# A two-layer encoder on one core: hi-weight products first, wide weight tiles, one kind of buffer, and an earlier gate convolution

## The chip, the cores and the metric

The kernel runs on one core of one Trainium2 chip. The metric is the device time of one execution in microseconds, the median of three runs. PE is the matrix engine (its weight loads are shown as PEld), ACT the scalar engine, DVE the vector engine, POOL the general one, and SP the queue that issues most transfers.

## The reference

Two layers on 256 tokens of width 2048, all in float32:

```
h = rms_norm(x, norm1_g[l])
q, k, v, gu, gv = jnp.split(h @ w_in[l], splits, axis=-1)
attn = banded_window_attention(q, k, v, sink[l])
sgu = chunked_spatial_gating(gelu(gu), gelu(gv), ...)
mixed = concatenate([rms_norm(attn, ...), rms_norm(sgu, ...)])
x = x + mixed @ w_o[l]
a = depthwise_conv_centred(rms_norm(x, norm2_g[l]) @ w_up[l], conv_w[l], conv_b[l])
g, u = jnp.split(a, 2, axis=-1)
x = x + (silu(g) * u) @ w_down[l]
```

The inner width of the last part is 5632, 44 tiles of 128 channels.

## The kernel before, in words

**Products in three parts.** PE multiplies in a fast 32-bit format that rounds its inputs. So each weight tile and each activation is split into a rounded part, hi, and the rest, lo, and a product is made of three: activation hi by weight hi, activation lo by weight hi, activation hi by weight lo. A block is four row tiles (KB = 4) of 512 weight columns: one transfer of 1 MB to `raw`, then `split_weights` has ACT round it to `hi` (L127) and DVE subtract it to `lo` (L111), each in two tiles of 1024 columns. `rows_by_cols` then issues 24 matmuls (L170), 128x512 each: for each of the four row tiles the four hi products (two halves of the tokens, two activation parts), then the two low ones.

**gu, the one projection made the other way.** `unit` takes the weights as the stationary operand and 256 channels a call: 32 hi products of 512 columns (L211), then 32 low ones of 256 (L216). `joined` then adds the two halves of its PSUM tile: ACT copies one (L227), DVE adds (L229). That frees the PSUM tile; there are three such tiles, `mm`.

**Stages of a layer.** Keys and queries, the second query group, gv in two chunks, gu in four units, with the steps of attention and of the spatial gating let in between; then w_o in two halves of four output columns; then up and down. In the last part the 44 tiles are worked off in two halves, 24 and 20. In each, `gate_and_up` makes for every four tiles a gate and an up product (L170 again); `leave` scales the result (L799), lays its 16-bit words apart (L801) and has the DMA queue transpose them; some blocks later `up_in` joins the words (L381), convolves gate and up (`convolved`, L781 to L785), multiplies and splits the result (`split_plain`, L242 and L243) into the list `ys`. Then four output columns of the down-projection run over `ys`, four tiles a block.

**What sets the order.** A scheduler orders the instructions of each engine when the program is made; each engine then works them off in that order and waits by semaphores. Weight splitting, joins and the like are `urgent`: first among what is ready. A tile of a pool can be taken only when an older tile of the pool has been released by its last reader; the scheduler places an instruction with that in view. Pools before: 58 general buffers `slots` of 2 KB a partition, 4 of the same size for evacuated results (`evp`), 4 for scratch (`scr`), 3 `raw` of 8 KB, 4 `hi` and 4 `lo` of 4 KB. `let_in` and `take` put waiting steps behind a given matmul.

## Time and profile before

| | us |
|---|---|
| median of three runs | 1971.58 |
| lowest, highest | 1971.37, 1972.12 |
| the profiled execution: its own time | 1971.57 |
| its span, first to last instruction | 1969.8 |
| PE busy | 1963.6 |
| ACT, DVE busy | 1316.6, 1256.4 |

The page is read as follows: a group of instructions has its line, engine, operation, output and inputs, shape and count, then its busy time and the mean of one in ns, then the engine's idle time just before them and what ended it. A timeline row has start, duration, engine, line, operation and count; times are us from the span's start. A waits row has the engine that waited, what for, the us in total, how often, and the longest.

### The profile page before, as it was taken

The page shows a single profiled execution, that of the slowest core. Times are in us where ns is not written, and L with a number is a line of the kernel's source. Part 1 is how long each engine was busy: PE and PEld are TensorE (multiplying, and loading weights), DVE is VectorE, ACT ScalarE, POOL GpSimd, SP SyncE. Part 2 cuts the span into 40 slices and gives each one's busy share as a digit, 9 for nine tenths or more (in the row PEclk, how much of TensorE's full clock was granted, in tenths as well). Part 3 has the DMA queues.
Part 4 walks back from the last instruction along what each step waited for, and adds up shares of the span by engine and source line. Part 5 has one row for each costly group of instructions (what it writes and reads, how often), then busy time and mean ns, then how long its engine had stood idle before and what let it go on. Part 6 is the DMA issues. An engine that isn't in the chain of part 4 may idle for free.

```text
span 1969.8 us, 23916 instructions
## 1 busy us (share of the span) xinstructions
PE 1963.6 (100%) x8880; PEld 1630.6 (83%) x8880; DVE 1256.4 (64%) x1754; ACT 1316.6 (67%) x1685; POOL 22.6 (1%) x25
## 2 busy tenths in 40 slices
PE   9999999999999999999999999999999999999999
PEld 8888888888888888888888888888888888888887
DVE  6779776666664456666567796666666544666664
ACT  6687487877753477777666864787777435777742
POOL 0100000000000000000000000000000000000000
PEclk9999999999999999999999999999999999999999
DMA  9764687777755677776667456867776556678763
GB/s 342 205 204 150 205 239 202 222 219 228 216 198 192 199 215 204 229 221 205 215 204 248 141 178 203 235 206 218 232 218 219 193 192 203 213 216 217 220 216 126
DMA packets 190741, 414.09 MB, mean 210 GB/s; under 512 B 139424, under 2 KB 140704, under 8 KB 145568
## 3 DMA queue, kind: packets, MB, share of 16 engines
q1 hardware_dynamic: 189904, 411.83, 67.2%
q8 instruction: 69, 1.13, 0.2%
q10 hardware_dynamic: 720, 0.73, 0.1%
q14 instruction: 48, 0.39, 0.1%
HBM read 378.43 MB, written 2.10 MB: 193 GB/s over the span
## 4 chain that ended last, share of the span: by engine, by line
PE 97%; DVE 2%; issue 0%; DMA 0%; SPq 0%; POOL 0%; ACT 0%; DVEq 0%
PE mm L170 91%; PE mm L211 2%; PE tp L170 1%; PE mm L216 1%; DVE lo L111 1%; PE tp L254 0%; PE tp L256 0%; PE tp L255 0%; PE tp L697 0%; PE tp L482 0%; DMA raw<-in_w_in 0%; DVE sl L235 0%; DVE xr L562 0%; SPq L87 0%; DVE sl L265 0%
## 5 line engine op out<-in xcount | busy, mean ns | idle before, releaser
L170 PE MATMUL mm<-hi,sl 128*128 128x512 f32 x5296 | 1418.4, 389 | 0.8 <-DVE sl L243 0.6
L111 DVE TENSOR_TENSOR lo<-raw,hi 128x1024 fp32r<-128x1024 f32 (+1 forms) x708 | 856.5, 1217 | 627.6 <-ACT hi L127 616.7
L170 PEld LDWEIGHTS mm<-hi,sl 128*128 128x128 f32 x5296 | 992.7, 188 | 208.2 <-DVE sl L243 1.5
L127 ACT ACTIVATE hi<-raw 128x1024 fp32r<-128x1024 f32 (+1 forms) x708 | 739.9, 1051 | 461.5 <-PE mm L170 426.0
L170 PE MATMUL mm<-lo,sl 128*128 128x512 f32 x2648 | 816.1, 389 | 0.0
L170 PEld LDWEIGHTS mm<-lo,sl 128*128 128x128 f32 x2648 | 496.9, 188 | 103.1
L381 ACT COPY sl<-sl 128x1024 uint16<-128x1024 uint16 x98 | 132.1, 1351 | 119.3 <-DMA sl<-sl 119.2
L781 ACT ACTIVATE sc<-sl,pc 128x256 f32<-128x256 f32 x176 | 97.0, 588 | 0.0
L801 ACT COPY sl<-ev 128x1024 uint16<-128x1024 uint16 x88 | 89.5, 1037 | 0.0
L782 DVE SCALAR_TENSOR_TENSOR sc<-sl,pc,sc 128x255 f32<-128x255 f32 x176 | 79.1, 479 | 2.6 <-ACT sc L781 2.6
L785 DVE SCALAR_TENSOR_TENSOR sc<-sl,pc,sc 128x255 f32<-128x255 f32 x176 | 79.1, 480 | 1.6
L211 PE MATMUL mm<-sl,hi 128*128 128x512 f32 x256 | 62.0, 391 | 0.0
L211 PEld LDWEIGHTS mm<-sl,hi 128*128 128x128 f32 x256 | 47.3, 188 | 9.3
L799 ACT ACTIVATE ev<-mm,yr 128x512 f32<-128x512 f32 x88 | 54.8, 672 | 0.0
L235 DVE SCALAR_TENSOR_TENSOR sl<-sl,pc 128x256 fp32r<-128x256 f32 x96 | 42.5, 479 | 16.9 <-ACT sl L234 16.9
L242 ACT ACTIVATE sl<-sl 128x256 fp32r<-128x256 f32 x88 | 32.1, 410 | 27.9 <-DVE sl L827 27.4
L234 ACT ACTIVATE sl<-sl,pc 128x256 fp32r<-128x256 f32 x96 | 43.0, 496 | 1.2 <-DMA pc<-in_pcol 0.6
L535 ACT COPY sl<-sl 128x1024 uint16<-128x1024 uint16 x24 | 32.4, 1349 | 6.8 <-DMA sl<-sl 6.8
L216 PE MATMUL mm<-sl,lo 128*128 128x256 f32 x256 | 34.2, 285 | 0.0
L243 DVE TENSOR_TENSOR sl<-sl 128x256 fp32r<-128x256 f32 x88 | 33.3, 419 | 0.0
L216 PEld LDWEIGHTS mm<-sl,lo 128*128 128x128 f32 x256 | 32.4, 191 | 0.6
L827 DVE TENSOR_TENSOR sl<-sl,sc 128x512 f32<-128x512 f32 x44 | 30.2, 686 | 0.2
(112 smaller groups left out, 582.7 us busy)
## 6 DMA issues: line engine op xcount, KB each, us to landing
raw<-in_w_up SPq DMA_DIRECT2D x176, 1024.0 KB, 5.0
raw<-in_w_down SPq DMA_DIRECT2D x88, 1024.0 KB, 4.9
raw<-in_w_in SPq DMA_DIRECT2D x38, 1024.0 KB, 5.3
raw<-in_w_o SPq DMA_DIRECT2D x32, 1024.0 KB, 5.0
raw<-in_w_gu SPq DMA_DIRECT2D x16, 1024.0 KB, 5.1
sl<-sl SPq DMA_TRANSPOSE x244, 3.6
sl<-in_prow SPq DMA_DIRECT2D x12, 256.0 KB, 7.0
raw<-in_w_in SPq DMA_DIRECT2D x8, 256.0 KB, 4.9
```

Source lines behind the costliest of these rows:

```text
L111: nc.vector.tensor_tensor(out=lo, in0=part, in1=hi.bitcast(F32), op=ALU.subtract)
L127: nc.scalar.activation(hi[:, cs], part, AF.Copy)
L170: nc.tensor.matmul(ps[m], acts[kk][:, part % 2, m * P : (m + 1) * P], w, start=first and kk == 0 and part == 0, stop=last and kk == KB - 1 ...
L211: nc.tensor.matmul(ps[:, i, :], tile_of(his, k, i), x1, start=k == 0, stop=False)
L216: nc.tensor.matmul(ps[:, i, :SEQ], tile_of(los, k, i), acts[k][:, 0, :], start=False, stop=k == NK - 1)
L234: nc.scalar.activation(t[:, 0, :], src, AF.Copy, scale=g)
L381: nc.scalar.copy(words, tall.rearrange("p (b a) n -> p b (a n)", b=2))
L781: nc.scalar.activation(t[:, i, :], s[:, i, :], AF.Identity, bias=col(3), scale=col(1))
L782: nc.vector.scalar_tensor_tensor(out=t[:, i, 1:], in0=s[:, i, : SEQ - 1], scalar=col(0), in1=t[:, i, 1:], op0=ALU.mult, op1=ALU.add)
L785: nc.vector.scalar_tensor_tensor(out=t[:, i, : SEQ - 1], in0=s[:, i, 1:], scalar=col(2), in1=t[:, i, : SEQ - 1], op0=ALU.mult, op1=ALU.add)
L799: nc.scalar.activation(rows, ps[:, m, :], AF.Copy, scale=r2[:, m : m + 1])
L801: nc.scalar.copy(h, rows.bitcast(U16).rearrange("p (j n b) -> p j b n", j=2, b=2))
```

## The change

The diff has five live parts.

1. **Order of the products.** In `rows_by_cols`, and in a new function `direct` for the down-projection, a block issues its 16 hi products first and its 8 low ones last. In `unit` the low products go row tile by row tile, the two channel halves in turn.
2. **Wide tiles.** `hi` and `lo` are one tile of 2048 columns a block, three `hi` and two `lo`; one rounding and one subtraction of 2048 columns take the place of two of 1024 (narrower for the first blocks of layer 0, by `step`).
3. **One kind of general buffer.** `evp` and `scr` are gone; what they held is taken from `slots`, now 62.
4. **Gate's convolution.** `gate_in` joins gate's words, convolves them and applies silu at once; `up_in` does the same for up alone.
5. **The halves and w_down.** The halves are 20 and 24 tiles. w_down lies in the order of its use, one long row a partition; the transfers keep their size.

New functions for a way of multiplying 2x2 blocks with seven products (`seven`, `seven_out`, `mixed`) come with it, but the table that would call for them, `FAST`, is empty, so none of it is issued.

```diff
+HALVES = ((0, 20), (20, NF))
+FAST = ((), ())
...
-    slots = pool("slots", 58)
-    evp = pool("evp", 4)
+    slots = pool("slots", 62)
     rawp = pool("rawp", 3)
-    hip = pool("hip", 4)
-    lop = pool("lop", 4)
-    scr = pool("scr", 4)
+    hip = pool("hip", 3)
+    lop = pool("lop", 2)
...
     def ev():
-        return evp.tile([P, 2, SEQ], F32, tag="ev", name="ev")
+        return sl([P, 2, SEQ])
 
     def sc(shape):
-        return scr.tile(shape, F32, tag="sc", name="sc")
+        return sl(shape)
...
+            hi, lo = hi_tile(), lo_tile()
+            for a in range(0, n, step):
+                cs = slice(a, min(a + step, n))
+                nc.scalar.activation(hi[:, cs], raw[:, cs], AF.Copy)
+                lo_part(lo[:, cs], raw[:, cs], hi[:, cs])
+        return hi, lo
...
                 product(m, kk, 0)
                 product(m, kk, 1)
-            for m in range(2):
-                product(m, kk, 2)
             if kk == 1:
                 let_in()
+        for kk in range(KB):
+            for m in range(2):
+                product(m, kk, 2)
...
-        for i in range(2):
-            for k in range(NK):
+        for k in range(NK):
+            for i in range(2):
                 nc.tensor.matmul(
                     ps[:, i, :SEQ], tile_of(los, k, i), acts[k][:, 0, :], start=False, stop=k == NK - 1
                 )
-                if i == 0 and k == 1:
-                    take(steps)
+            if k == 0:
+                take(steps)
...
+            step = 4 * W if l or b > 1 else W if raw is not None else 2 * W
+            rows_by_cols(ps, acts[b * KB : b * KB + KB], src, b == 0, b == NB - 1, raw, step=step)
...
             def gate_in(tall):
-                g.extend(together(t) for t in tall)
+                for i in range(2):
+                    g = together(tall[i])
+                    y = sl([P, 2, SEQ])
+                    nc.scalar.activation(y, convolved(g, 4 * j + 2 * i), AF.Silu)
+                    gs.append(y)
...
-                    y = sl([P, 2, SEQ])
-                    nc.scalar.activation(y, convolved(g[i], f), AF.Silu)
-                    t = convolved(u, NF + f)
+                    y = gs[i]
+                    t = convolved(u, NF + 4 * j + 2 * i)
...
-        for f0, f1 in ((0, 24), (24, NF)):
-            ys = []
+        w_at = 0
+        for half, (f0, f1) in enumerate(HALVES):
+            ys, plain = [], {}
...
-                    src = w_down[l, c, :, k * W : (k + KB) * W]
-                    rows_by_cols(ps, ys[k - f0 : k - f0 + KB], src, k == f0, k + KB == f1, None, end and k + KB == f1)
...
+                    src = w_down[l, :, w_at : w_at + len(cs) * len(ks) * W]
+                    w_at += len(cs) * len(ks) * W
+                    acts = [ys[k - f0] for k in ks]
...
+                    direct(sums[c], acts, src, fresh[c], finished, end and finished)
```

Lines move with the change: L170 is now L185 (L213 in `direct`), L127 is L158, L111 is L146, L211 and L216 are L329 and L334, L227 and L229 are L345 and L347, L242 and L243 are L360 and L361, L249 is L367, L482 is L600.

**PE, the first two blocks of the program** (`mm` is the PSUM tile, `sl` the activations). Before:

```order
L170 MATMUL mm<-hi,sl 128x512 x4
L170 MATMUL mm<-lo,sl 128x512 x2
L170 MATMUL mm<-hi,sl 128x512 x4
L170 MATMUL mm<-lo,sl 128x512 x2
L170 MATMUL mm<-hi,sl 128x512 x4
```

Now:

```order
L124 MATMUL tp<-ones 128x128 x10
L185 MATMUL mm<-hi,sl 128x512 x16
L185 MATMUL mm<-lo,sl 128x512 x8
L185 MATMUL mm<-hi,sl 128x512 x16
L185 MATMUL mm<-lo,sl 128x512 x8
```

The low products of all four row tiles have moved behind the last hi one.

**DVE, layer 0, where gu ends and w_o begins** (`lo_...` are low weights, those of 1024 or 2048 columns; `ev_1662<-mm_1549`, `sl_1456<-mm_1321` are joins of gu units). Before, at the end of the third unit, `mm_1549`:

```order
L714 TENSOR_SCALAR sl_1235<-sl_1235,mv_1239,lnr_1244 128x512
L111 TENSOR_TENSOR lo_1695<-raw_1692,hi_1694 128x1024
L111 TENSOR_TENSOR lo_1699<-raw_1692,hi_1698 128x1024
L229 TENSOR_TENSOR ev_1662<-mm_1549,ev_1660 128x512
L111 TENSOR_TENSOR lo_1705<-raw_1702,hi_1704 128x1024
L687 TENSOR_TENSOR ev_1662<-ev_1662,rb_750 128x512
L111 TENSOR_TENSOR lo_1709<-raw_1702,hi_1708 128x1024
```

Now, at the end of the fourth unit, `mm_1601`; `mm_1321` is the second one:

```order
L146 TENSOR_TENSOR lo_1744<-raw_1741,hi_1743 128x2048
L586 TENSOR_TENSOR rs_1393<-rs_1393,es_1391 128x4
L383 TENSOR_TENSOR sl_489<-sl_489,sl_1415 128x512
L146 TENSOR_TENSOR lo_1790<-raw_1787,hi_1789 128x2048
L347 TENSOR_TENSOR sl_1456<-mm_1321,sl_1454 128x512
L588 RECIPROCAL rec_1400<-rs_1393 128x4
L353 SCALAR_TENSOR_TENSOR sl_1418<-sl_1413,pc_83,sl_1418 128x256
L806 TENSOR_TENSOR sl_1456<-sl_1456,rb_708 128x512
L592 TENSOR_SCALAR sl_1370<-sl_1370,rec_1400 128x256 x2
L592 TENSOR_SCALAR sl_1380<-sl_1380,rec_1400 128x256 x2
L353 SCALAR_TENSOR_TENSOR sl_1421<-sl_1413,pc_83,sl_1421 128x256
L367 TENSOR_TENSOR sl_1520<-tp_1514,sl_1519 128x512
```

The join of the second unit has moved from the second unit's end to the fourth's, behind two low tiles. `lo_1744` and `lo_1790` take over the buffers of `lo_1605` and `lo_1611`, so they wait for PE's last product on these. On PE the same place reads now (`[waits ...]` names the engine whose semaphore the row waits for):

```order
L334 MATMUL mm_1601<-sl_225,lo_1605 128x256 x2
L334 MATMUL mm_1601<-sl_299,lo_1611 128x256 x2
L334 MATMUL mm_1601<-sl_302,lo_1611 128x256 x2
L334 MATMUL mm_1601<-sl_307,lo_1611 128x256 x2
L334 MATMUL mm_1601<-sl_310,lo_1611 128x256 x2
L334 MATMUL mm_1601<-sl_375,lo_1611 128x256 x2
L334 MATMUL mm_1601<-sl_378,lo_1611 128x256 x2
L334 MATMUL mm_1601<-sl_383,lo_1611 128x256
L600 MATMUL tp_1523<-ident_116,sl_1230 128x128 [waits Activation_49]
L600 MATMUL tp_1523<-ident_116,sl_1230 128x128
L600 MATMUL tp_1523<-ident_116,sl_1240 128x128 x2
L334 MATMUL mm_1601<-sl_383,lo_1611 128x256
```

Behind these rows stand the last two low products on `lo_1611` and then the first of w_o, `mm_1740<-hi_1743,sl_1159`, which waits for the join of `mm_1321`.

**PE, layer 0, the end of the first up-projection** (`mm_4023` and `mm_4212` are the first two output columns of the down-projection, `sl_4142` is the first of the last four `y`, `hi_4182` its weights). Now:

```order
L213 MATMUL mm_4212<-hi_4215,sl_2846 128x512 [waits Activation_49]
L213 MATMUL mm_4212<-hi_4215,sl_2846 128x512 x2
L213 MATMUL mm_4023<-hi_4182,sl_4142 128x512 [waits Activation_49]
L213 MATMUL mm_4212<-hi_4215,sl_2846 128x512
L213 MATMUL mm_4212<-hi_4215,sl_2849 128x512 x4
L213 MATMUL mm_4212<-hi_4215,sl_2862 128x512 x4
L213 MATMUL mm_4023<-hi_4182,sl_4142 128x512 [waits DVE_49]
L213 MATMUL mm_4023<-hi_4182,sl_4142 128x512 x2
```

Before, the same place in the second half, the one with five blocks (`sl_7465` and `sl_7468` are the last two `y`):

```order
L170 MATMUL mm_7292<-hi_7485,sl_7440 128x512 x4
L170 MATMUL mm_7292<-lo_7486,sl_7440 128x512 x2
L170 MATMUL mm_7292<-hi_7485,sl_7443 128x512 x4
L170 MATMUL mm_7292<-lo_7486,sl_7443 128x512 x2
L170 MATMUL mm_7292<-hi_7489,sl_7465 128x512 x4
L170 MATMUL mm_7292<-lo_7490,sl_7465 128x512 x2
```

The products of the second output column have moved in between those of the first that need the last `y`.

## The prediction

> **What bounds the kernel now.** I read the cores first, then the page, then PE's timeline, then the waits.

> ```profile
> core 0: 1969.8 us, clock 1.000
> ...
> PE 1963.6 (100%) x8880; PEld 1630.6 (83%) x8880; DVE 1256.4 (64%) x1754; ACT 1316.6 (67%) x1685; POOL 22.6 (1%) x25
> ...
> PE 97%; DVE 2%; issue 0%; DMA 0%; SPq 0%; POOL 0%; ACT 0%; DVEq 0%
> ```

> TensorE runs at its full granted clock, is busy through the span, and carries 97% of the chain that ends last. But a busy PE need not be PE at its pace, so the pace comes from start times:

> ```profile
> 599.83 1.07 PE L170 MATMUL mm<-hi,sl 128*128 128x512 f32 x4
> 600.73 0.61 PE L170 MATMUL mm<-lo,sl 128*128 128x512 f32 x2
> 601.18 1.07 PE L170 MATMUL mm<-hi,sl 128*128 128x512 f32 x4
> ```

> Four hi products start in 0.90 us and two low ones in 0.45, so a product costs 0.226 us whether its weights are hi or low. A block of 24 takes 5.4 us. The program has the same 8880 records after the change and each keeps its shape; only what PE loses between them can move the time. The weight loads' waits say how much that is:

> ```profile
> PEld tp L254 <- issue: 2.1, 5, 0.8
> PEld mm L170 <- DVE sl L243: 1.5, 2, 0.8
> ...
> PEld mm L170 <- ACT hi L127: 0.9, 2, 0.6
> PEld mm L170 <- ACT sl L234: 0.8, 2, 0.4
> ```

> With the rows left out (0.7 and less each, the warm-up's own row aside) these come to some 7.3 us. That is all that a change of order and buffers can win, 0.37% of the span; what it can lose has no such bound.

> **The change part by part.** The sum is made against the profiled execution, 1971.57 us, which lies at the median of the runs, 1971.58.

> *Wide tiles.*

> ```profile
> L127 ACT ACTIVATE hi<-raw 128x1024 fp32r<-128x1024 f32 x700 | 734.8, 1056 | 459.6 <-PE mm L170 426.0 <-PE tp L170 10.0 <-PE mm L211 6.7
> ...
> L111 DVE TENSOR_TENSOR lo<-raw,hi 128x1024 fp32r<-128x1024 f32 x700 | 851.1, 1223 | 625.5 <-ACT hi L127 614.7 <-PE mm L170 9.8 <-PE mm L216 0.4
> ...
> L111 DVE TENSOR_TENSOR lo<-raw,hi 128x512 fp32r<-128x512 f32 x8 | 5.4, 692 | 2.0 <-ACT hi L127 2.0
> ```

> 512 more columns cost DVE 1.223 - 0.692 = 0.53 us, so a subtraction of 2048 takes 1.223 + 1.06 = 2.29 us against two of 1.22. That saves 0.16 us of DVE a block, over 342 blocks 55 us, and ACT gains likewise. Both sit beside PE at 64% and 67%, so I count the saving as nothing. In the steady stretches three wide hi tiles and two wide low ones hold as many columns as before or more: a low buffer is free at the end of block n-2, its content is needed 16 products into block n, which leaves 5.4 + 3.6 = 9.0 us for 2.29. Nothing is lost there. If that cover were gone, a block would lose part of 2.29 us.

> *Hi products first, in the head.*

> ```profile
> 1.05 4.43 PE L98 MATMUL tp<-ones 128*128 128x128 f32 x20 [1.05 <-DVE ones L94]
> ...
> 6.07 0.63 ACT L127 ACTIVATE hi<-raw 128x512 fp32r<-128x512 f32 x1 [1.03 <-DMA raw<-in_w_in]
> ...
> 7.86 0.63 ACT L127 ACTIVATE hi<-raw 128x512 fp32r<-128x512 f32 x1 [0.54 <-DMA raw<-in_w_in]
> ...
> 8.55 1.19 PE L170 MATMUL mm<-hi,sl 128*128 128x512 f32 x4
> 8.88 3.27 ACT L127 ACTIVATE hi<-raw 128x512 fp32r<-128x512 f32 x5
> ...
> 11.40 1.07 PE L170 MATMUL mm<-hi,sl 128*128 128x512 f32 x4
> ```

> The first weights land in four pieces, and their hi parts end at 6.70, 8.49 (PE starts 0.06 later) and 8.88 + 0.63 = 9.51. Before, the two low products of each piece fill PE's time until the next one; the second block starts at 11.40. Now PE runs four hi products (0.9 us) and waits: the third piece goes 8.55 to 9.46, the fourth 9.57 to 10.48, and then come all eight low ones, 1.81 us, until 12.29. That is **+0.9 us**. It can be less, down to 0, if later waits of the loading phase fall into that lead.

> *The ends of the up-projections.*

> ```profile
> 901.75 0.39 PE L170 MATMUL mm<-hi,sl 128*128 128x512 f32 x1
> ...
> 902.38 0.96 PE L170 MATMUL mm<-hi,sl 128*128 128x512 f32 x3 [0.25 <-DVE sl L243]
> ...
> 1881.06 0.39 PE L170 MATMUL mm<-hi,sl 128*128 128x512 f32 x1
> 1881.83 0.96 PE L170 MATMUL mm<-hi,sl 128*128 128x512 f32 x3 [0.38 <-DVE sl L243]
> ```

> In each layer's second half the down-projection has only five blocks per output column, and the fifth waits for the last `y`, which DVE splits (L243). The first gap is 0.63 against 0.23, the second 0.77; three products then take 0.96 instead of 0.84. Together 0.52 + 0.66 = 1.2 us. The second halves now have 24 tiles, a block (5.4 us) more lead, and gate's convolution is done one joining earlier, so these two waits go. The first halves now have the five blocks, but there the order shows PE going on with the next output column before the last `y`, as shown above: **-1.2 us**. If the new boundary waits as the old one did, 0.

> *One kind of general buffer.* This is the part that costs. The join of a gu unit (L227/L229, now L345/L347) frees the unit's PSUM tile. Before, its two buffers came from a pool of their own, and the join stood right behind its unit. Now they come from the 62 general ones, and in layer 0 the join of the second unit (`mm_1321`) stands behind the low tile `lo_1790`, whose buffer PE frees only with the last low product of the fourth unit. The very next matmul, the first of w_o (`mm_1740`), waits for that join. All of it is in the rows above. What the steps take is read from the same kinds of steps before:

> ```profile
> 161.54 0.68 DVE L229 TENSOR_TENSOR ev<-mm,ev 128x512 f32<-128x512 f32 x1
> 162.14 1.21 DVE L111 TENSOR_TENSOR lo<-raw,hi 128x1024 fp32r<-128x1024 f32 x1
> 163.27 0.68 DVE L687 TENSOR_TENSOR ev<-ev,rb 128x512 f32<-128x512 f32 x1
> 163.87 1.22 DVE L111 TENSOR_TENSOR lo<-raw,hi 128x1024 fp32r<-128x1024 f32 x1
> 165.01 0.15 DVE L468 TENSOR_TENSOR rs<-rs,es 128x4 f32<-128x4 f32 x1
> 165.08 0.68 DVE L265 TENSOR_TENSOR sl<-sl,sc 128x512 f32<-128x512 f32 x1
> 165.68 0.17 DVE L470 RECIPROCAL rec<-rs 128x4 f32<-128x4 f32 x1
> 165.77 0.45 DVE L235 SCALAR_TENSOR_TENSOR sl<-sl,pc 128x256 fp32r<-128x256 f32 x1
> 166.14 1.14 DVE L474 TENSOR_SCALAR sl<-sl,rec 128x256 f32<-128x256 f32 x4
> 167.19 0.48 DVE L235 SCALAR_TENSOR_TENSOR sl<-sl,pc 128x256 fp32r<-128x256 f32 x1
> 167.59 1.52 DVE L249 TENSOR_TENSOR sl<-tp,sl 128x512 fp32r<-128x512 f32 x2
> ```

> DVE takes its instructions in order, each starting 0.08 before the one ahead has ended (162.14 + 1.21 against 163.27). `lo_1744` starts when the last low product on its buffer ends, 0.3 us after that product's start. Then: 2.2 for `lo_1744`, 0.07, 0.60, 2.2 for `lo_1790`, 0.68 for the join, 0.05 to hand over, 6.1 us in all. PE meanwhile has 17 low products and four transposes:

> ```profile
> 171.24 0.48 PE L216 MATMUL mm<-sl,lo 128*128 128x256 f32 x2
> 171.72 0.66 PE L482 MATMUL tp<-ident,sl 128*128 128x128 f32 x4
> 172.14 3.47 PE L216 MATMUL mm<-sl,lo 128*128 128x256 f32 x27
> ...
> 208.26 0.39 PE L170 MATMUL mm<-lo,sl 128*128 128x512 f32 x1
> 209.00 0.41 PE L282 MATMUL tp<-ident,sl 128*128 128x128 f32 x2 [0.35 <-DVE sl L276]
> ```

> At 0.12 a low product (27 in 3.47) and 0.42 for four transposes that is 2.5 us, so PE stands for 6.1 - 2.5 = 3.6 us. Eleven matmuls on (2.5 us) it needs the split of a transposed probability tile (L367), which stands behind the join, the reciprocal, two splits, the next gate product and four scalings: 0.60 + 0.09 + 0.37 + 0.60 + 1.05 + 0.40 + 0.69 = 3.8, against 0.68 + 2.5: 0.6 more. The new waits cost **+4.3 us**. Behind so long a pause some old ones go: the gap of 0.74 at 208.26 (0.5 too many) and that of 0.48 at 171.24 (0.24 too many), **-0.75**. The bounds are +3.1 (PE's last low product, `lo_1790` and the join alone) with all other waits of the stage gone, and +4.3 with none gone.

> *Layer 1.* Joins stand late there too, but the PSUM tile that w_o takes is freed over 50 matmuls ahead, and the attention steps are spread wider. I take 0. The bounds are -0.7, a layer's share of the issue row (2.1 in five waits) gone, and +2.1, two places where a wide subtraction stands ahead of something that PE needs (2.2 instead of 1.14 each).

> *Not counted:* w_down read from another layout (transfers of the same size and number, three raw buffers ahead of PE); low products of a gu unit alternating between two banks (same 0.12); the sevenfold code, which never runs.

> [...]

> Sum: 0.9 - 1.2 + 4.3 - 0.75 = **+3.25 us**, 1974.8.

> **The rivals.**
> - *The pause is filled* (0.12): ACT and DVE run ahead of what the rows allow, or the late join hides in waits that PE had anyway. Then 0.9 - 1.2 and about 1 are left: 1972.3. For it: the stage's old waits lie close together. Against it: `lo_1790` waits for PE itself.
> - *More places of this kind* (0.14, slower): general buffers run out in layer 1 or in the attention steps too, so two or three more subtractions of 2.2 us stand ahead of PE's input. It decides from two such places: 3.25 + 2 x 2.2, 1979.2. Against it: the order shows no other matmul so soon behind its release.
> - *The clock drops in the pause* (0.06, slower): the profile's first matmuls run slow, 20 of 128 columns in 4.4 us, where later four transposes of that width take 0.42. If a pause of 3.6 us brings that back, some 4 us run at half pace, +2: 1976.9. No pause of the trace is as long (0.8 at most), and the clock row is 1.000. [...]
> - *The waits go and no pause comes* (0.03): 7.3 us are all there is; half of them gone gives 1967.5.

> **How the numbers follow.** My forecast has 0.65: 1974.8, by its bounds 1972.6 to 1977.5. What a measurement of this kernel tells from no change is 0.2%, 3.9 us, that is 1975.5; the forecast's part below it is 0.45, above it 0.20. With the rivals: faster 0.03, same 0.57, slower 0.40. The range runs from 1971.5, which takes in most of the filled pause, to 1978.5.

> **What would show it.** Right: one gap on PE of 3 to 4 us at about 172 us, ended by DVE L347, with a 128x2048 subtraction just ahead of it; gaps at 11 us as worked out; none at the ends of the up-projections; 0.226 a product elsewhere. Wrong: no such gap, or PE's pace changed inside the blocks, or waits on `hi` or `raw` in the steady stretches.

## The result and the profile after

The changed kernel takes 1981.01 us (median of six runs, 1979.59 to 1982.28) against 1971.68 for the kernel before on the same chip. The ratio is 1.0047, 95% interval 1.0034 to 1.0060: it is slower by 9.3 us, and 2.5 us beyond the upper end of the forecast range.

The profile shown is that of a run of 1982.28 us, 10.71 above the profiled run of before. First the cores, the page's first part and its chain:

```profile
core 0: 1980.6 us, clock 0.999
...
PE 1967.8 (99%) x8880; PEld 1631.2 (82%) x8880; DVE 1226.9 (62%) x1412; ACT 1289.8 (65%) x1345; POOL 19.7 (1%) x25
...
PE 94%; DMA 2%; DVE 2%; ACT 1%; issue 1%; SPq 0%; POOL 0%; DVEq 0%; ACTq 0%
```

PE has the same 8880 records. DVE and ACT do less than before (1226.9 against 1256.4, 1289.8 against 1316.6): the subtractions alone fell from 856.5 to 807.0, near the 55 less of the forecast, and it is worth nothing. The mean clock is no longer 1.000, and DMA has come into the chain. The waits of PE's weight loads name the places:

```profile
PEld mm L185 <- DVE sl L347: 3.7, 1, 3.7
PEld tp L372 <- ACT sl L366: 2.7, 3, 1.2
PEld mm L185 <- ACT hi L158: 2.2, 3, 1.3
PEld mm L213 <- ACT sl L360: 1.2, 3, 0.7
PEld tp L372 <- ACT sl L609: 1.2, 1, 1.2
```

One wait of 3.7 us is the forecast pause; the others were not in the sum, or smaller. On PE's and DVE's timelines the pause looks like this:

```profile
175.00 0.60 PE L334 MATMUL mm<-sl,lo 128*128 128x256 f32 x3
179.11 4.01 PE L185 MATMUL mm<-hi,sl 128*128 128x512 f32 x11 [3.51 <-DVE sl L347]
182.91 1.48 PE L816 MATMUL tp<-sl 128*128 128x128 f32 x8
```

```profile
173.28 2.29 DVE L146 TENSOR_TENSOR lo<-raw,hi 128x2048 fp32r<-128x2048 f32 x1 [1.84 <-PE mm L334]
175.49 0.16 DVE L586 TENSOR_TENSOR rs<-rs,es 128x4 f32<-128x4 f32 x1
175.57 0.68 DVE L383 TENSOR_TENSOR sl<-sl 128x512 f32<-128x512 f32 x1
176.17 2.28 DVE L146 TENSOR_TENSOR lo<-raw,hi 128x2048 fp32r<-128x2048 f32 x1
178.37 0.68 DVE L347 TENSOR_TENSOR sl<-mm,sl 128x512 f32<-128x512 f32 x1
```

That is the forecast step, instruction by instruction: 2.29 was estimated for a wide subtraction, 2.29 measured. But the eleven products behind the pause take 4.01 us instead of 2.5, and a window over six of them has a granted clock of half (each row: the stretch, its length, then busy time and count for PE, PEld, DVE, ACT and POOL, the clock, the DMA share, GB/s):

```profile
179.00:180.50 1.50, 1.39 (x6) 1.17 (x7) 1.50 (x6) 0.35 (x1) 0.00 (x0) 0.96 0.99 317
180.50:182.90 2.40, 2.40 (x7) 1.83 (x6) 2.26 (x6) 1.73 (x4) 0.00 (x0) 0.50 0.88 372
```

Where the 10.7 us are, comes from PE's start times: from the gap between two starts I take the pace of the first one (0.2267 us for 512 columns, 0.1175 for 256, 0.109 for 128), and add up what is left by stage. It is PE's loss in us, of the profiled execution of each kernel (the five lower rows are experiments of the next section):

| kernel | head (first 64 records) | projections | layer 0 up to w_o | w_o and on, layer 0 | last part, layer 0 | layer 1 up to the last part | last part, layer 1 |
|---|---|---|---|---|---|---|---|
| before | 2.7 | 0.3 | 2.0 | 1.1 | 0.5 | 2.0 | 0.6 |
| changed | 4.4 | 0.0 | 3.8 | 6.4 | 0.1 | 4.7 | 0.6 |
| order alone | 3.8 | 0.3 | 2.1 | 0.8 | -0.1 | 12.1 | -0.1 |
| one pool alone | 2.5 | 0.3 | 4.1 | 6.9 | 1.2 | 2.1 | 1.2 |
| wide tiles and one pool | 2.9 | 0.0 | 10.4 | 1.0 | 18.7 | 4.5 | 24.5 |
| changed, joins' own pool | 3.7 | 0.0 | 5.0 | 2.8 | 0.1 | 3.6 | 0.3 |
| the same, old order in the head | 2.8 | 0.7 | 2.3 | 2.8 | 0.1 | 3.8 | 0.2 |

The steady stretches of the last part lose nothing in either kernel (the new layout of w_down, which was not run alone, is read there). The change lost at its seams: the head, the stretch from attention to w_o in both layers, and the start of w_o.

### The profile page after: what moved, and what is told of

Its sections match the earlier page's. It is cut to its first block, busy times and chain, and to the rows that moved or that the text cites. A ratio compares the mean times of both kernels' runs of the same rounds, so it can differ in the third digit from the quotient of the medians.

```text
span 1980.6 us, 22857 instructions
## 1 busy us (share of the span) xinstructions
PE 1967.8 (99%) x8880; PEld 1631.2 (82%) x8880; DVE 1226.9 (62%) x1412; ACT 1289.8 (65%) x1345; POOL 19.7 (1%) x25
## 4 chain that ended last, share of the span: by engine, by line
PE 94%; DMA 2%; DVE 2%; ACT 1%; issue 1%; SPq 0%; POOL 0%; DVEq 0%; ACTq 0%
PE mm L185 66%; PE mm L213 22%; PE mm L329 2%; PE tp L213 2%; PE mm L334 1%; DMA raw<-in_w_gu 1%; DVE lo L146 1%; DMA sl<-sl 1%; ACT hi L158 0%; PE tp L816 0%; PE tp L372 0%; PE tp L600 0%; PE tp L374 0%; PE tp L373 0%; DMA raw<-in_w_in 0%
## 5 line engine op out<-in xcount | busy, mean ns | idle before, releaser
L146 DVE TENSOR_TENSOR lo<-raw,hi 128x2048 fp32r<-128x2048 f32 (+2 forms) x366 | 807.0, 2209 | 579.8 <-PE mm L185 364.0
L158 ACT ACTIVATE hi<-raw 128x2048 fp32r<-128x2048 f32 (+2 forms) x366 | 676.0, 1849 | 483.5 <-PE mm L185 177.9
L185 PE MATMUL mm<-hi,sl 128*128 128x512 f32 x3968 | 945.4, 390 | 4.6 <-DVE sl L347 3.5
L185 PEld LDWEIGHTS mm<-hi,sl 128*128 128x128 f32 x3968 | 744.6, 188 | 160.1 <-DVE sl L347 3.7
L185 PE MATMUL mm<-lo,sl 128*128 128x512 f32 x1984 | 491.6, 389 | 0.4 <-DVE lo L146 0.4
L185 PEld LDWEIGHTS mm<-lo,sl 128*128 128x128 f32 x1984 | 371.8, 188 | 77.7 <-DVE lo L146 0.8
L213 PE MATMUL mm<-hi,sl 128*128 128x512 f32 x1312 | 311.6, 389 | 0.3 <-ACT sl L360 0.3
L213 PEld LDWEIGHTS mm<-hi,sl 128*128 128x128 f32 x1312 | 246.0, 188 | 52.4 <-ACT sl L360 1.2
L499 ACT COPY sl<-sl 128x1024 uint16<-128x1024 uint16 x98 | 132.4, 1351 | 133.9 <-DMA sl<-sl 133.9
L213 PE MATMUL mm<-lo,sl 128*128 128x512 f32 x656 | 162.4, 389 | 0.0
L213 PEld LDWEIGHTS mm<-lo,sl 128*128 128x128 f32 x656 | 123.1, 188 | 25.5
L901 DVE SCALAR_TENSOR_TENSOR sl<-sl,pc 128x255 f32<-128x255 f32 x176 | 80.4, 480 | 31.4 <-ACT sl L900 31.1
L900 ACT ACTIVATE sl<-sl,pc 128x256 f32<-128x256 f32 x176 | 95.6, 591 | 1.5
L920 ACT COPY sl<-sl 128x1024 uint16<-128x1024 uint16 x88 | 92.1, 1047 | 2.8
L904 DVE SCALAR_TENSOR_TENSOR sl<-sl,pc 128x255 f32<-128x255 f32 x176 | 77.2, 478 | 0.3
L329 PE MATMUL mm<-sl,hi 128*128 128x512 f32 x256 | 63.3, 395 | 0.0
L918 ACT ACTIVATE sl<-mm,yr 128x512 f32<-128x512 f32 x88 | 59.7, 678 | 0.0
L329 PEld LDWEIGHTS mm<-sl,hi 128*128 128x128 f32 x256 | 46.9, 188 | 9.1
L678 DVE TENSOR_TENSOR xr<-mm,xr 128x512 f32<-128x512 f32 x24 | 15.5, 686 | 38.0 <-PE mm L213 38.0
L653 ACT COPY sl<-sl 128x1024 uint16<-128x1024 uint16 x24 | 32.3, 1346 | 7.6 <-DMA sl<-sl 7.6
```

The lines of the kernel that those rows point to most:

```text
L146: nc.vector.tensor_tensor(out=lo, in0=part, in1=hi.bitcast(F32), op=ALU.subtract)
L158: nc.scalar.activation(hi[:, cs], raw[:, cs], AF.Copy)
L185: nc.tensor.matmul(ps[m], acts[kk][:, part % 2, m * P : (m + 1) * P], w, start=first and kk == 0 and part == 0, stop=last and kk == KB - 1 ...
L213: nc.tensor.matmul(ps[m], acts[kk][:, part % 2, m * P : (m + 1) * P], w, start=first, stop=done and kk == len(acts) - 1 and part == 2,)
L329: nc.tensor.matmul(ps[:, i, :], tile_of(his, k, i), x1, start=k == 0, stop=False)
L499: nc.scalar.copy(words, tall.rearrange("p (b a) n -> p b (a n)", b=2))
```

## The experiments

Times are medians; "before" ran on the same chip each time and stood at 1971.7 to 1971.8.

**1. Joins and evacuated results with a pool of their own** (changed kernel):

```diff
-    slots = pool("slots", 62)
+    slots = pool("slots", 58)
+    evp = pool("evp", 4)
...
 def ev():
-    return sl([P, 2, SEQ])
+    return evp.tile([P, 2, SEQ], F32, tag="ev", name="ev")
```

> The changed kernel with one edit: joins and evacuated results get their own pool of 4 back, general buffers 58 instead of 62 (the same room in all). Theory A (the join of the second gu unit waits for a general buffer, so it falls behind two wide subtractions; the six half-speed products after the pause are its follow-up): the pause of 3.7 us at 175 us goes, and the half-speed products with it (1.4), 1981.0 - 5.1 = 1975.9; the small waits in front of the transposes (L372) stay. Rival B (the wide subtractions alone hold the join up, whichever pool it takes its buffer from): a pause of 2 us or more stays at the start of w_o, 1979 or more.

Measured: 2021.64, far from both. The pause at w_o did go (loss there 1.9 instead of 6.4), as theory A says. But the last part lost 25.0 and 23.5 us: with 58 buffers for all the rest the transposes land later, and ACT, which joins the words, waits 183.4 us for them instead of 133.9. That they lack a free buffer is the likely reason; no run shows which tile they wait for. The row is the group of these joins, before it comes the same of the changed kernel:

```profile
L499 ACT COPY sl<-sl 128x1024 uint16<-128x1024 uint16 x98 | 132.4, 1351 | 133.9 <-DMA sl<-sl 133.9
```

```profile
L500 ACT COPY sl<-sl 128x1024 uint16<-128x1024 uint16 x98 | 132.2, 1349 | 183.4 <-DMA sl<-sl 183.4
```

The wide tiles take 40 KB a partition where the narrow ones took 32, so four buffers are missing, and the common pool has that many less.

**2. A pool of two for the joins alone**, in which they add in place; 60 buffers for all else:

```diff
+    evj = pool("evj", 2)
...
 def joined(ps):
-        rest = ev()
+        rest = evj.tile([P, 2, SEQ], F32, tag="ev", name="ev")
         nc.scalar.copy(rest, ps[:, :, SEQ:])
-        s = ev()
-        nc.vector.tensor_tensor(out=s, in0=ps[:, :, :SEQ], in1=rest, op=ALU.add)
-    return s
+        nc.vector.tensor_tensor(out=rest, in0=ps[:, :, :SEQ], in1=rest, op=ALU.add)
+    return rest
```

> The changed kernel with one edit: only the joins of the gu units get a pool of their own, 2 buffers, and add in place; all else shares the other 60. Theory A: the pause and its half-speed products go, 1981.0 - 5.1 = 1975.9, if 60 buffers still carry the last part. The run with 58 for all but the evacuated results lost 24 us a layer there, because the transposes (SP) had no buffer to go to; if that loss goes with the number of buffers, 60 would lose up to half of it: 1975.9 + 24 = 2000.

Measured: 1977.43 (1975.99 to 1978.08, nine runs): 3.6 us of 9.3 back. Neither the pause nor a half-speed product is left, and the last part loses nothing with 60. On PE's timeline the first product of w_o now stands right behind the last low product of gu:

```profile
172.25 4.00 PE L335 MATMUL mm<-sl,lo 128*128 128x256 f32 x32
176.08 5.19 PE L186 MATMUL mm<-hi,sl 128*128 128x512 f32 x21
```

The gain is 1.5 less than expected; in the profiled run two other waits are longer (1.9 us at 112.6, 1.0 at 217.7). That the late join was a question of buffers is shown.

**3. The pause filled.** Twenty products with zero weights, 256 columns each, are added at the end of the fourth gu unit of layer 0; they change no sum:

```diff
+    zero = const.tile([P, P], F32R, tag="zero", name="zero")
+    nc.scalar.activation(zero, ones, AF.Copy, scale=0.0)
...
 def unit(acts, w, steps=(), fill=0):
...
+        for n in range(fill):
+            nc.tensor.matmul(ps[:, n % 2, :SEQ], zero, acts[n % NK][:, 0, :], start=False, stop=n >= fill - 2)
```

> The changed kernel with 20 products more: the fourth gu unit of layer 0 ends with 20 products of 256 columns whose weights are all zero, 2.4 us at 0.12 each. They stand in the pause before w_o; what DVE does there, and when the join frees the PSUM tile, stays. Clock theory (the products at half speed behind the pause come from PE standing still for 3.8 us): idle time falls to 1.4 us, no product at 0.427 follows, 1981.0 - 1.4 (between 1.2 and 2.4) = 1979.6, and the runs spread less. Rival (what follows the pause is slow for another reason, such as the transfers or DVE's work at that time): 1981.0, half-speed products as before.

Measured: 1978.52, 2.5 us faster than the changed kernel with more work on PE. The join frees the tile as late as before, and what follows runs at full pace:

```profile
176.05 2.52 PE L342 MATMUL mm<-sl,zero 128*128 128x256 f32 x20
179.72 3.96 PE L187 MATMUL mm<-hi,sl 128*128 128x512 f32 x16 [1.16 <-DVE sl L351]
```

```profile
180.00:182.00 2.00, 2.00 (x10) 1.59 (x10) 2.00 (x7) 1.24 (x3) 0.00 (x0) 1.00 0.97 332
```

Sixteen products in 3.96 us where eleven took 4.01, under the same load of transfers (332 GB/s here, 317 and 372 there). So the half clock came from PE standing still: 3.51 us there, 1.16 here. The runs spread as much as before (1977.2 to 1980.3), against the expectation; experiment 7 shows one reason.

**4. One pool alone**, in the kernel before: `evp` and `scr` go into `slots`, 66 of them.

```diff
-    slots = pool("slots", 58)
-    evp = pool("evp", 4)
+    slots = pool("slots", 66)
...
-    scr = pool("scr", 4)
...
```

> The kernel before with one part of the change alone: one kind of general buffer, 66 of them (the room of 58 + 4 + 4), narrow tiles, products in the old order. Theory A (common buffers make the joins of the gu units late): the join that w_o waits for stands behind narrow subtractions, a pause of 2.0 to 2.5 us at the start of w_o in layer 0, no half-speed products after it, 1971.8 + 2.4 = 1974; if the small waits of layer 1 are of this kind too, 1976.5. Rival C (only wide tiles bring waits): 1972.

Measured: 1981.96, 10.2 us slower than before, and more than any theory gave it. The mechanism of theory A is there with narrow tiles and with no buffer lost, and it is not alone: the waits are a join again, gu's PSUM tile (L209) for ACT's evacuation, and the last `y` (L240, L241) at the four boundaries.

```profile
PEld tp L252 <- issue: 3.6, 5, 1.9
PEld mm L168 <- DVE sl L227: 2.6, 1, 2.6
PEld mm L168 <- DVE sl L241: 1.9, 4, 0.7
PEld mm L209 <- ACT sl L667: 1.6, 1, 1.6
PEld mm L168 <- ACT sl L240: 1.6, 2, 0.8
```

After the pause of 2.5 us seven products ran at half speed here too, which was not expected. Layer 1 up to its last part lost 2.1, as before: the common pool by itself does not cost there.

**5. The order alone**, in the kernel before:

```diff
                 product(m, kk, 1)
-            for m in range(2):
-                product(m, kk, 2)
             if kk == 1:
                 let_in()
+        for kk in range(KB):
+            for m in range(2):
+                product(m, kk, 2)
```

> The kernel before with one part of the change alone: a block's 16 hi products first, its 8 low ones last (narrow tiles, own pools, the unit's order as before). Theory D (the order of the products brings the new small waits): the head costs 1.0 to 1.6 us as in the changed kernel, and layer 1 between its query groups and w_o some 2 us more: 1971.8 + 3.3 = 1975. Rival C (the waits of layer 1 come with the wide tiles or the common buffers): only the head, 1973.

Measured: 1981.68, 9.9 us slower, more than either theory gave it. The head lost 1.1 more, and layer 1 12.1 us instead of 2.0, most of it in three pauses of 1.5 to 3.0 us. None of the three is there in the changed kernel, so the 9.9 is not the order's share of its loss. In the longest, PE waits for a split (L250) that stands on DVE behind two subtractions and a step of the gating:

```profile
1165.57 1.97 PE L170 MATMUL mm<-lo,sl 128*128 128x512 f32 x8
1170.40 0.50 PE L256 MATMUL tp<-sl 128*128 128x512 f32 x1 [2.85 <-DVE sl L250]
```

```profile
1166.79 2.35 DVE L111 TENSOR_TENSOR lo<-raw,hi 128x1024 fp32r<-128x1024 f32 x2
1169.06 0.69 DVE L717 TENSOR_TENSOR sl<-sl 128x512 f32<-128x512 f32 x1
1169.66 0.69 DVE L250 TENSOR_TENSOR sl<-tp,sl 128x512 fp32r<-128x512 f32 x1
```

**6. Wide tiles and one pool, products in the old order** (kernel before; `hi` 3, `lo` 2, 62 buffers, `split_weights` as in the changed kernel):

```diff
-    hip = pool("hip", 4)
-    lop = pool("lop", 4)
+    hip = pool("hip", 3)
+    lop = pool("lop", 2)
...
```

> The kernel before with two parts of the change: wide tiles (3 hi, 2 low) and one kind of general buffer, 62 of them; products in the old order. Theory A + C (buffers and width bring the waits, the order none): head as before, layer 1 some 2 us more, a pause at the start of w_o only if the join is late in this order too, which the order of the instructions does not show: 1971.8 + 2 to 4, 1975. Theory D (the order brings them): 1972.

Measured: 2024.12, 52 us slower, which no theory had. 46 waits for the low part:

```profile
PEld mm L157 <- DVE lo L118: 36.9, 46, 3.6
```

In the old order a block needs its low part four products in; two low buffers, each held to the end of its block, don't allow that. So wide tiles with two low buffers can't be had without the new order, and the order by itself costs 9.9. Layer 1 up to its last part loses 4.5 here and 4.7 in the changed kernel, against 2.1 with one pool and narrow tiles: in the old order that loss comes with the wide tiles (and four buffers fewer, 62 for 66). One place is the same in both kernels with wide tiles and in neither of experiments 4 and 5: a wide rounding waits for its transfer, an attention step stands behind it on ACT, and PE loses 0.8 us in the changed kernel (first row) and 0.7 here (second).

```profile
1119.00 1.91 ACT L158 ACTIVATE hi<-raw 128x2048 fp32r<-128x2048 f32 x1 [1.12 <-DMA raw<-in_w_gu]
1136.41 1.91 ACT L130 ACTIVATE hi<-raw 128x2048 fp32r<-128x2048 f32 x1 [1.02 <-DMA raw<-in_w_gu]
```

The new order and the common pool with narrow tiles were not run together. The parts don't add up (9.9 and 10.2 alone, 9.3 for the whole change): the scheduler finds another order of instructions for each kernel, so neither is that part's share of the 9.3.

**7. Half-width instructions** on the wide tiles (changed kernel):

```diff
             hi, lo = hi_tile(), lo_tile()
+            step = min(step, 2 * W)
             for a in range(0, n, step):
```

> The changed kernel with one edit: the hi and low tiles stay 2048 wide, but each is rounded and subtracted in two instructions of 1024 columns. Theory B (a short step of attention or gating that PE waits for stands behind a rounding of 1.9 or a subtraction of 2.3 us): most of the small waits beyond those of before go (layer 0 ahead of the pause 1.6, layer 1 2.6 us), and the pause shrinks by some 2 us, too short for half-speed products: 1981.0 - 3 - 2 - 1.4, about 1975. Theory A (the buffers set the waits, not the width): only the pause shrinks, 1977.5 to 1979, and the waits in front of L372 stay.

Measured: 1985.66, slower than the changed kernel. The pause shrank only to 3.1 us, layer 1 lost 4.8 as before, and a new wait of 2.9 came at its first boundary. The timeline of DVE at the pause shows why nothing was won there: both halves become ready at the same time, so they still run in one stretch.

```profile
171.77 4.63 DVE L146 TENSOR_TENSOR lo<-raw,hi 128x1024 fp32r<-128x1024 f32 x4 [1.86 <-PE mm L335]
176.32 0.68 DVE L348 TENSOR_TENSOR sl<-mm,sl 128x512 f32<-128x512 f32 x1
```

So what was ready together ran together, in two instructions a tile (four in 4.63 us) as in one (2.29 and 2.28). What changed is seen in the waits of DVE and ACT, in the whole run, of before (L111, L127) and of the changed kernel (L146, L158):

```profile
DVE lo L111 <- ACT hi L127: 616.7, 399, 6.2
DVE lo L111 <- PE mm L170: 9.8, 5, 3.1
...
ACT hi L127 <- DMA raw<-in_w_in: 7.5, 7, 2.8
ACT hi L127 <- DMA raw<-in_w_gu: 2.0, 2, 1.4
```

```profile
DVE lo L146 <- PE mm L185: 364.0, 179, 3.2
DVE lo L146 <- PE mm L213: 140.0, 52, 3.2
...
ACT hi L158 <- DMA raw<-in_w_o: 32.4, 11, 9.7
ACT hi L158 <- DMA raw<-in_w_down: 30.2, 11, 8.3
ACT hi L158 <- DMA raw<-in_w_gu: 22.1, 8, 4.7
```

Before, a subtraction waited for its rounding and for hardly anything else (9.8 us for PE): its buffer was free. Now it waits for PE to finish the low products at the end of a block. The raw buffer is held as long, the next transfer starts later, and the rounding waits for the transfer, with the short steps of attention queued behind it on ACT. Added up over all weights, the roundings wait for transfers 9.5 us in the kernel before, 7.3 with one pool alone, 11.1 with the order alone, 36 with wide tiles in the old order (experiment 6) and 109 in the changed kernel: the late transfers come with the wide tiles, and the new order adds to them. One such place on ACT's timeline, in the changed kernel and in the one of experiment 8b, whose instructions are the same up to there:

```profile
110.52 1.92 ACT L158 ACTIVATE hi<-raw 128x2048 fp32r<-128x2048 f32 x1 [4.39 <-DMA raw<-in_w_gu]
112.34 1.34 ACT L499 COPY sl<-sl 128x1024 uint16<-128x1024 uint16 x1
113.72 0.63 ACT L366 ACTIVATE sl<-sl 128x512 fp32r<-128x512 f32 x1
```

```profile
109.19 1.92 ACT L158 ACTIVATE hi<-raw 128x2048 fp32r<-128x2048 f32 x1 [3.47 <-PE mm L185]
111.01 1.34 ACT L499 COPY sl<-sl 128x1024 uint16<-128x1024 uint16 x1
112.38 0.63 ACT L366 ACTIVATE sl<-sl 128x512 fp32r<-128x512 f32 x1
```

Where the transfer has landed in time, PE waits 0.3 us for L366, otherwise 1.2 (here and in experiment 8a), and 2.1 in the run of experiment 3. The transfer took 6.3 us from issue to landing, 7.5 in the changed kernel and 8.4 in experiment 3; why it varies stays open. These four executions have one order of instructions there, so this place can make up a good part of the changed kernel's spread.

**8. The halves (a) and the gate convolution (b) undone**, each alone in the changed kernel, and **made in the kernel before**, the convolution alone (c) and with the halves (d):

```diff
-HALVES = ((0, 20), (20, NF))
+HALVES = ((0, 24), (24, NF))
```

> The changed kernel with one edit: the halves are 24 and 20 tiles again (w_down laid out for it). If the halves are what took away the waits at the two second boundaries (0.4 and 0.5 us before the change), these come back, and the new wait at the first boundary of layer 1 (0.5 us) goes: 1981.0 + 0.4 = 1981.4. If the earlier gate convolution took them away, they stay away and the new wait goes: 1980.5.

Measured: 1980.63, no difference that can be told from the changed kernel's 1981.01. The wait at the first boundary of layer 1 went, and none came back at the second ones (last part 0.0 and 0.0 us).

```diff
                 for i in range(2):
-                    g = together(tall[i])
-                    y = sl([P, 2, SEQ])
-                    nc.scalar.activation(y, convolved(g, 4 * j + 2 * i), AF.Silu)
-                    gs.append(y)
+                    gs.append(together(tall[i]))
...
-                    y = gs[i]
+                    y = sl([P, 2, SEQ])
+                    nc.scalar.activation(y, convolved(gs[i], 4 * j + 2 * i), AF.Silu)
```

> The changed kernel with one edit: gate's words are only joined when they come; its convolution and silu are done with up's again. If the earlier convolution is what shortened the way to the last y, PE waits 0.4 to 0.7 us more at each of the four boundaries of the down-projection: 1981.0 + 2 = 1983. If the halves alone did it: 1981.0, and no other wait than before at the boundaries.

Measured: 1984.98, 4.0 us more, with waits for the last `y` of 1.4, 1.3 and 1.5 us at three boundaries. So in the changed kernel the earlier convolution, not the halves, keeps the boundaries clear. In the kernel before it was then to be a gain by itself (the two texts are those of c and d):

> The kernel before with one part of the change alone: gate's convolution and silu when its words are joined (halves 24 and 20, pools, tiles and order as before). If the earlier convolution takes away the waits at the ends of the up-projections, as undoing it in the changed kernel suggests, the 0.4 and 0.5 us at the two second boundaries go: 1971.8 - 0.9 = 1970.9. If not: 1971.8.

> As the run before, with halves of 20 and 24 tiles too. If the halves add nothing, as undoing them in the changed kernel showed: 1970.9; if they only move the wait to the first boundaries: 1971.8.

Measured: 1974.03 (eleven runs, 1971.78 to 1975.19) and 1980.32 (1972.99 to 1982.00), medians slower than before by 2.3 and 8.6, though both have runs near the kernel before. The conclusion doesn't carry over: with the old buffers and order the boundaries get worse, in the second kernel by one wait of 3.7 us for the last `y` with seven products at half speed behind it:

```profile
1495.50 0.49 PE L170 MATMUL mm<-hi,sl 128*128 128x512 f32 x1 [3.51 <-ACT sl L242]
1496.52 1.30 PE L170 MATMUL mm<-hi,sl 128*128 128x512 f32 x3 [0.53 <-DVE sl L243]
```

Why the order that the scheduler finds is worse there, stays open.

**9. The old order in the head alone**, on the kernel of experiment 2: the first two blocks issue their low products row tile by row tile.

```diff
                 product(m, kk, 1)
+            if step == W:
+                for m in range(2):
+                    product(m, kk, 2)
             if kk == 1:
                 let_in()
-        for kk in range(KB):
+        for kk in range(KB if step > W else 0):
```

> The changed kernel with the joins' own pool (2 buffers, 60 others) and the old order of products in the first two blocks of the program only. If the head's loss is the order of the products while the first weights land, PE's loss in the first 64 products falls from 3.7 to 2.7 us: 1977.4 - 1.0 = 1976.4. If it is the transfers themselves: 1977.4.

Measured: 1976.17 (eleven runs, 1974.68 to 1977.55), 1.3 less; the head's loss falls from 3.7 to 2.8. Behind it 0.7 comes back, most of it in one wait for a split at 19 us. What is gained besides stands in layer 0 ahead of w_o (2.3 instead of 5.0), where the transfer at 110 us had landed in time. So this pair alone does not price the head; all fourteen profiled executions do: head and projections together lose 2.8 to 3.5 us in the six with the old order there, 3.7 to 4.4 in the eight with the new. This is the best of the changed kernel's relatives, still 4.4 us behind the kernel before, which no other kernel here beat.

## Why the prediction was wrong

By its own steps, in us (measured: the table by stage, profiled executions):

| step | forecast | measured |
|---|---|---|
| hi first, in the head | +0.9 | +1.6, then -0.3 behind it |
| boundaries | -1.2 | -0.4 |
| pause at w_o (with 0.6 at L367) | +4.3 | +3.7 |
| half clock behind it | a rival, 0.06 | +1.6 (six products 1.2, eight transposes 0.4) |
| old waits swallowed | -0.75 | 0.0 in w_o: the 0.5 at 208 us went, small new ones took its place |
| layer 0 ahead of w_o | 0 | +1.8 (-0.3 to +2.3 in four executions with one order there) |
| layer 1 | 0 | +2.6 |

- **The pause was right** in its place, its cause, its price and its releaser; experiments 2 and 4 show the general buffers behind it. The 0.6 more at L367 was not to be seen, since PE came there later, at half speed.
- **The step that failed is that of the wide tiles**: "I count the saving as nothing", "Nothing is lost there", and zero for layer 1. The lead of 9.0 us was worked out for the steady blocks, and holds there. But it was held against PE alone. Where the sum had nothing, layer 0 ahead of w_o lost 1.8 more and layer 1 2.6. The stretch from attention to w_o lives on ACT and DVE finishing short steps between blocks, and there the subtraction's new wait for PE, the raw buffer held by it and the late transfer push them back, as the places at 113 us in layer 0 and 1121 us in layer 1 show. That the late transfers come with the wide tiles is shown (9.5 us of waits before, 36 and 109 with them). Experiments 4 and 6 put layer 1's loss on these tiles in the old order; how the 2.6 divide between tiles and order in the changed kernel stays open, and so does whether it is the whole tile's release or the two halves' running together.
- **The clock** was listed with a condition, "a pause of 3.6 us brings that back", that the forecast itself met. The trace of before did not show it (no pause between its products was over 0.8 us), so the condition and the price of +2 were the author's estimate. The runs showed it: +1.6, and experiment 3 its cause.
- **The head** had the right mechanism (experiment 9) and somewhat too small a size: +1.4 net of what came back behind it in this execution, 1.1 of it in one wait for a piece of the weights.
- **The boundaries** gave a third of what was forecast: the old waits went, in the changed kernel by the convolution and not by the halves (experiments 8a, 8b), but a new one of 0.5 came at 1497.9, which the bound "if the new boundary waits as the old one did" had allowed.
- **The bounds** were added up too low: the upper ones of the text, 0.9, 0, 4.3 and 2.1, give 7.3 and 1978.9, not 1977.5. That is still 2.1 us short, for want of the half clock and of any term for layer 0 ahead of w_o.

The rival "more places of this kind" (1979.2) was nearest to the time, which was luck: its reason was further general buffers, and the runs show late transfers and the half clock.

## What to carry to other kernels

A part of a change that "takes no time" where one engine is saturated still sets when a buffer comes free (here the roundings' waits for transfers went from 9.5 to 109 us with PE 99% busy): ask, for each in-order queue, what the instruction at its head now waits for that it didn't wait for before, and what short step stands behind it. Merging pools is such a part too: with the same room in all it cost 10.2 us by itself. And a pause of the matrix engine is to be priced with what follows it, half-speed products above all: products with zero weights that filled 2.4 us of one were a gain of 2.5.

## What the runs showed of the hardware

Products of 512 columns ran at 0.427 us instead of 0.227, at a granted clock of 0.50, after each of the eleven pauses of PE of 3.3 us or more in these fourteen traces (3.7 us in the changed kernel, up to 7.2 in experiment 1). Shorter pauses went both ways: those of 2.2 (experiment 6), 2.5 (experiment 4), 2.9 (experiment 7, layer 1) and 3.0 us (experiment 5) were followed by slow products, one of 3.0 (experiment 7, layer 0) and six of 2.0 to 2.5 in experiment 1 were not.

```profile
180.40:183.80 3.40, 3.40 (x12) 2.82 (x11) 2.36 (x6) 1.83 (x4) 0.00 (x0) 0.50 0.65 270
177.40:184.20 6.80, 6.11 (x17) 5.05 (x18) 4.34 (x12) 2.08 (x4) 0.00 (x0) 0.50 0.62 234
```

PE's loss, reckoned as in the table by stage and added up by steps of this grid, parts the cases without an exception: of the 8058 steps at full clock, the 15 in which PE lost 2.05 us or more were followed by a step at half clock, and the 8043 in which it lost 1.89 us or less were not. The pause of 3.0 us in experiment 7 fell across two steps with at most 1.89 in one; that of 2.2 us in experiment 6 lay in one, which lost 2.5 in all. So some 2 us of lost time within one step of 3.41 us were enough here.
